# A two-layer fp32 transformer trunk on one core: layer 0's first output tokens loaded into the old pool, the last projection cut into six single tiles and five pairs, and layer 1's conditioning tied to its slots

## The chip, the cores and the metric

The kernel runs on one core of one Trainium2 chip. The metric is device time in microseconds (us) of one execution, given as the median of several runs. Besides, one execution was taken with the hardware profiler; its timeline is the source of all times of single instructions.

The engines are named as in the profile: PE is TensorE (matrix products), DVE is VectorE, ACT is ScalarE, POOL is GpSimd, SP is SyncE, which here does nothing but issue DMAs. SPq is SP's queue. "L247" is line 247 of the kernel before.

## The reference

One inference step of a trunk of two layers over 640 tokens of width 2048: 512 latent tokens and 128 context tokens. Each layer does this (the mixers' insides are left out):

```
for layer in (0, 1):
    shift, scale, gate = split(silu(cond) @ ada_w[layer] + ada_b[layer], 3)
    h = rms_norm(x, norm_g) * (1 + scale) + shift
    p = h @ w_in[layer]                     # the input projection
    o = concat(mixer 1(p), mixer 2(p))      # attention, gated conv
    o = o * silu(gate paths of p)
    x = x + gate * (o @ w_out[layer])       # the output projection
```

Layer 0 mixes with a banded attention and a gated convolution, layer 1 with a differential attention and an attention with rotary positions. `cond` has two rows, one for the latent tokens and one for the context tokens, so "conditioning" below means two products of a vector with a 2048 x 6144 matrix in each layer. Everything is fp32. The result is x of the last layer, with the context tokens' new keys and values.

## The kernel before, in words

**Tiles and products.** Tokens lie along the free axis in two halves of 320, features along the partitions in 16 blocks k of 128. An fp32 product is made of three fp32r products: each operand is split into a high part and a low part (`split`, L215 on ACT for the high part and L216 on DVE for the low one), and TensorE adds hi x hi, hi x lo and lo x hi (L247, L248, L249 in `proj_q`). An output tile is 128 features x 640 tokens in two PSUM banks (`pa`, `pb`): 16 blocks x 3 products x 2 halves = 96 matmuls. Its weights come in four quarters of four blocks each (256 KB), loaded by SP (`load_raw`, L228, tile `raw`) and split (`split_w`, tiles `wh` and `wl`); the pool of these tiles has four buffers of each, so a load waits for an older split and a split for matmuls that are done with its buffer. Within a tile, a quarter is 24 matmuls.

**The order of the work.** The program is written as Python generators that take turns: `run_tiles` walks through the tiles of a projection, and at the end of each quarter calls `slot`, which advances whatever is queued (`prep`: what follows a finished tile; `attn`: an attention head or the forms below; `fill`: a conditioning block). A scheduler then orders the instructions of each engine by its own model of time, so that neighbouring pieces of work may change places, where buffers and data allow it. Pools of tiles are opened and closed by hand; a tile in a new pool must wait for the old pool's tiles that lay there.

**Leads.** The first three tiles of a projection are leads (`run_tiles`, first loop). They run side by side through the quarters, because the tokens' blocks are made only now: before a quarter's matmuls, `make_h(k)` loads and splits block k. In the output projection the quarters are taken in the order 0, 2, 1, 3.

**The output projection** (`project_out`). It has 16 tiles n. Three are leads; one more, number N_SINGLE-1, is done singly, its token half 1 first and half 0 afterwards; the other 12 tiles are done as six pairs (`run_pairs`). A pair computes two tiles with seven products of half the depth and half the tokens instead of eight: 7 x 24 = 168 matmuls (L494, L495, L496, tile `pq`) against 192 for two single tiles. For it, sums of token blocks are needed, the forms: `forms` (L1018 on) loads blocks j and j+8 once more from DRAM (`w<-yd`, L1028), makes three sums and one more of them on DVE and splits the three into tiles T0 to T7. It is a generator with eight steps in the queue `attn`. The fourth sum (`t1`) is split in place over the tokens' half 1 when the fourth single tile's half 1 is done. The pairs' weights come in half columns (`load8`, L406, tag `w8`, four buffers); the forms' loads use the same four buffers.

**The tokens of the output projection.** The attention and the gates leave their results y (16 blocks) in DRAM as `yd` (`save_y`, L794, on POOL's queue). `y0_maker` (L1134) is layer 0's `make_h`: at k = 0 it closes the pool "even", opens "mid", allocates two tiles for the norm's sums, and starts the forms; `late_yin` (L1062, load at L1064) then loads each block into one of three buffers with the tag `xr` in the new pool and splits it. Layer 1's counterpart `y1_maker` already loads blocks 0 to 3 and 8 to 11 into buffers of the old pool (L1375). `y_maker` (L797) makes such a function for given tags of the pool that is current. In layer 0's attention the tags q0h, q0l, q1h and q1l hold the split q of the heads.

**What follows a tile.** In layer 1, each finished tile is added to the residual (L1059), then `rows_out` transposes it back to rows (L523 on PE, five transposes), copies it (L1381) and writes it out.

**Conditioning.** Layer 1's last four blocks of conditioning columns are made on DVE while layer 1's input projection runs (`ada_on_dve`, called `fill1`): for each block, 64 multiply-adds of half width (L187, in two accumulators `acc0` and `acc1`; the weights `adaw` loaded at L181 in three buffers), summed over the partitions by PE at the end (L193). `slot` advances the block by FILL1 = 0.9 steps a quarter from the 24th quarter on. Nothing but the buffers holds a block's DVE operations at the place where they are written.

**Layer 1's heads.** When a key tile is done, its rows are transposed on PE, squared on ACT (L548), scaled and rotated on DVE (L550 to L568, tile `m`), and transposed back on PE (L523).

Of the kernel before, what the change touches and what calls it, by code (L numbers as in the profile page):

```python
# [20 lines left out]
P = 128  # L21
D = 2048
KT = D // P
# [30 lines left out]
def trunk_kernel(ctx: ExitStack, tc: tile.TileContext, I: dict, O: dict):  # L54
# [114 lines left out]

    def ada_on_dve(blocks, tags, parts=1):  # L170

        wt, wd = tags[2:5], 512 // parts
        bufs = 3 if wt[0] == wt[1] else 1
        for l, cb in blocks:
            ap = pools["cur"]
            acc = [ap.tile([P, 512], F32, tag=tags[c], name=f"acc{c}", bufs=1) for c in range(2)]
            for i in range(KT * parts):
                kt, h = i % KT, i // KT
                w = ap.tile([P, wd], F32, tag=wt[i % 3], name="adaw", bufs=bufs)
                c0 = cb * 512 + h * wd  # L180
                nc.sync.dma_start(w, I["ada_w"][l, kt * P:(kt + 1) * P, c0:c0 + wd])  # L181
                for c in range(2):
                    a = acc[c][:, h * wd:(h + 1) * wd]
                    if kt == 0:
                        V.tensor_scalar(a, w, sT[:, kt, c:c + 1], None, ALU.mult)
                    else:
                        V.scalar_tensor_tensor(out=a, in0=w, scalar=sT[:, kt, c:c + 1], in1=a,  # L187
                                               op0=ALU.mult, op1=ALU.add)
                yield
# [36 lines left out]
    def load_raw(w_ap, col, qd, js=(0, 4)):  # L226
# [3 lines left out]
        return raw  # L230

    def split_w(raw):
        wh = wpool.tile(raw.shape, F32R, tag="wh", name="wh")
        wl = wpool.tile(raw.shape, F32R, tag="wl", name="wl")
        split(wh, wl, raw)
        return wh, wl

# [544 lines left out]
    fill0 = ada_on_dve(ada_rest[:N_FILL0], ("acc0", "acc1", "adaw", "adaw", "adaw", "z"))  # L782
    fill1 = ada_on_dve(ada_rest[N_FILL0:], ("acc0", "acc1", "adaw", "adaw", "adaw", "adaw"), 2)

# [225 lines left out]

    N_SINGLE = 4
    room = [tables[:, i * HALF:(i + 1) * HALF] for i in range(4)]
# [61 lines left out]
    def project_out(l, maker, finish, last, tail):  # L1074
# [11 lines left out]

        go_on = run_tiles([(n * P, job(n)) for n in range(N_SINGLE - 1)], w, maker, order=(0, 2, 1, 3))

        n = N_SINGLE - 1
        parts = [split_w(load_raw(w, n * P, qd)) for qd in range(4)]  # L1090
        go_on()
        pp = new_pp(0)
        for hv in (HV[1:], HV[:1]):
            for qd in range(4):
                proj_q(pp, parts[qd], qd, qd, hv)
                advance(attn, 2)
                go_on()
            if hv == HV[1:]:
                drain(attn)
                for j in range(8):  # L1100
                    hi, lo = hs[j]
                    split(hi[:, HALF:NT], lo[:, HALF:NT], t1[j])
        while go_on():
            pass
        prep.append(job(n)(pp))
        advance(prep, 1)

# [4 lines left out]
        def begin(p):  # L1112
            for t in range(2):
                res_load(l, N_SINGLE + 2 * p + t)

        def part(p, t, h, src):
            res_sum(l, N_SINGLE + 2 * p + t, src, CS[1:] if h else CS[:1])

        seen = set()

        def done(p, t, h, src):
            n = N_SINGLE + 2 * p + t
            part(p, t, h, src)
            if n >= KT - 2:
                last(t, h)
            elif n in seen:
                prep.append(later(n))
            seen.add(n)

        run_pairs([(n * P, (n + 1) * P) for n in range(N_SINGLE, KT, 2)], w,  # L1130
                  {"B11": half_of(0, 0), "T1": half_of(0, 1), "B21": half_of(8, 0), "B22": half_of(8, 1),
                   "T2": form_of(0), "T3": form_of(1), "T4": form_of(2)}, room, begin, part, done, tail)
        drain(prep)


    def y0_maker(k):
        if k == 0:
            close("even")
# [320 lines left out]
```

## Time and profile before

| what | value |
|---|---|
| runs | 2344.29, 2342.13, 2342.52 us |
| median | 2342.52 us |
| the profiled execution | 2347.92 us |
| its span (first to last instruction) | 2345.9 us |
| granted TensorE clock, mean | 0.994 of full speed |
| TensorE busy | 2286.9 us (97% of the span), 15900 matmuls |
| DVE, ACT, POOL busy | 67%, 40%, 6% |
| DMA | 321.92 MB, mean 137 GB/s |

How to read it: the times in the prediction's rows are counted from the span's start. A row of the timeline has start, duration, engine, line, operation, what is written `<-` what is read, and in brackets how long the engine had been idle before, and whose end it waited for. A row "x3" stands for three instructions one after the other. A row of the stretches has the busy time of each engine with its number of instructions, then the granted clock and the DMA engines' share and rate. A matmul's duration is longer than its distance to the next one, because they are pipelined.

Layer 0's output projection begins at about 921 us, layer 1's loads its first tokens from 2112 us on. Layer 1's input projection begins at about 1145 us.

### The profile page before, as it was taken

How to read it: one execution, taken by the hardware profiler on the slowest of the kernel's cores; microseconds unless marked ns; L12 is line 12 of the kernel's file. 1: busy time of each engine (PE TensorE's matmuls, PEld its weight loads, DVE VectorE, ACT ScalarE, POOL GpSimd, SP SyncE). 2: the span in 40 equal slices, each digit the busy share in tenths (PEclk: the TensorE clock that was granted, in tenths of full speed). 3: DMA queues.
4: the chain of work that ended last, by engine and by line, in shares of the span. 5: the costliest groups of instructions: out<-in, count | busy, mean ns of one | idle time of the engine just before them, and what ended most of it. 6: DMA issues, size and time to landing. Idle time of an engine off the chain costs nothing.

```text
span 2345.9 us, 41233 instructions
## 1 busy us (share of the span) xinstructions
PE 2286.9 (97%) x15900; PEld 2207.9 (94%) x15900; DVE 1577.8 (67%) x3187; ACT 932.9 (40%) x1934; POOL 129.7 (6%) x175
## 2 busy tenths in 40 slices
PE   6999999999999998999999999999999999999999
PEld 3789999999999998999989999999999999999999
DVE  4458886786866663888886445755855754568776
ACT  4325442433422222544553443444334444445343
POOL 0001000000000000000010100101000001000101
PEclk9999999999999999999999999999999999999999
DMA  9984545435355544844442222413423312128542
GB/s 325 327 266 141 157 117 170 138 117 170 106 172 155 154 136 127 274 140 129 157 135 84 80 74 71 139 55 97 120 72 92 106 46 82 46 74 282 165 122 69
DMA packets 386209, 321.92 MB, mean 137 GB/s; under 512 B 18033, under 2 KB 327854, under 8 KB 385502
## 3 DMA queue, kind: packets, MB, share of 16 engines
q1 hardware_dynamic: 378448, 290.96, 40.7%
q0 software_dynamic: 7024, 28.12, 3.3%
q8 instruction: 125, 2.05, 0.4%
q14 instruction: 70, 0.57, 0.1%
q10 hardware_dynamic: 542, 0.22, 0.0%
HBM read 290.79 MB, written 28.44 MB: 136 GB/s over the span
## 4 chain that ended last, share of the span: by engine, by line
PE 87%; DMA 5%; DVE 4%; issue 2%; ACT 2%; SPq 1%; POOL 0%; ACTq 0%; DVEq 0%; POOLq 0%
PE pa L247 10%; PE pb L247 10%; PE pb L248 10%; PE pb L249 10%; PE pa L248 10%; PE pa L249 10%; PE pq L494 4%; PE pq L496 4%; PE pq L495 4%; PE T L672 2%; DMA yin<-yd 2%; PE S L684 1%; PE S L686 1%; PE S L685 1%; DMA ada<-in_ada_w 1%
## 5 line engine op out<-in xcount | busy, mean ns | idle before, releaser
L215 ACT ACTIVATE wh<-raw 128x512 fp32r<-128x512 f32 (+1 forms) x478 | 298.5, 625 | 792.0 <-PE pb L248 655.0
L247 PE MATMUL pa<-h,wh 128*128 128x320 f32 x1728 | 552.0, 320 | 10.6 <-ACT h L215 7.9
L216 DVE TENSOR_TENSOR wl<-raw,wh 128x512 fp32r<-128x512 f32 (+1 forms) x478 | 326.5, 683 | 348.3 <-ACT wh L215 321.7
L248 PE MATMUL pa<-h,wh 128*128 128x320 f32 x1728 | 538.5, 312 | 2.8 <-DVE h L216 2.8
L249 PE MATMUL pa<-h,wl 128*128 128x320 f32 x1728 | 536.3, 310 | 0.0
L247 PE MATMUL pb<-h,wh 128*128 128x320 f32 x1728 | 535.8, 310 | 0.0
L249 PE MATMUL pb<-h,wl 128*128 128x320 f32 x1728 | 535.7, 310 | 0.0
L248 PE MATMUL pb<-h,wh 128*128 128x320 f32 x1728 | 535.1, 310 | 0.0
L187 DVE SCALAR_TENSOR_TENSOR acc<-adaw,sT,acc 128x512 f32<-128x512 f32 (+1 forms) x600 | 358.2, 640 | 16.3 <-DMA adaw<-in_ada_w 15.6
L247 PEld LDWEIGHTS pa<-h,wh 128*128 128x128 f32 x1728 | 326.5, 189 | 30.1 <-issue 14.9
L248 PEld LDWEIGHTS pa<-h,wh 128*128 128x128 f32 x1728 | 327.2, 189 | 8.5 <-issue 4.2
L249 PEld LDWEIGHTS pb<-h,wl 128*128 128x128 f32 x1728 | 325.0, 188 | 2.9 <-issue 2.9
L249 PEld LDWEIGHTS pa<-h,wl 128*128 128x128 f32 x1728 | 326.2, 189 | 1.3 <-issue 1.2
L247 PEld LDWEIGHTS pb<-h,wh 128*128 128x128 f32 x1728 | 325.3, 188 | 0.9 <-issue 0.4
L248 PEld LDWEIGHTS pb<-h,wh 128*128 128x128 f32 x1728 | 325.1, 188 | 0.1
L658 ACT ACTIVATE p<-S,nm,rq 128x768 f32<-128x768 f32 (+3 forms) x120 | 101.3, 844 | 114.2 <-DVE nm L653 80.0
L496 PE MATMUL pq<-h,wl 128*128 128x320 f32 x384 | 119.2, 311 | 3.1 <-DVE wl L216 3.1
L494 PE MATMUL pq<-h,wh 128*128 128x320 f32 x384 | 120.5, 314 | 0.3 <-DVE xr L1059 0.3
L495 PE MATMUL pq<-h,wh 128*128 128x320 f32 x384 | 119.1, 310 | 0.0
L651 DVE TENSOR_REDUCE nm<-S 128x1 f32<-128x768 f32 (+3 forms) x120 | 92.0, 767 | 16.0 <-PE S L686 14.9
L215 ACT ACTIVATE pth<-T 128x512 fp32r<-128x512 f32 (+1 forms) x132 | 66.2, 533 | 72.5 <-PE T L672 72.5
L495 PE MATMUL pq<-T,wh 128*128 128x320 f32 x288 | 88.8, 308 | 0.0
(294 smaller groups left out, 3446.6 us busy)
## 6 DMA issues: line engine op xcount, KB each, us to landing
raw<-in_od_w_in SPq DMA_DIRECT2D x208, 256.0 KB, 2.8
raw<-in_ev_w_in SPq DMA_DIRECT2D x202, 256.0 KB, 3.0
adaw<-in_ada_w SPq DMA_DIRECT2D x192, 256.0 KB, 2.9
ada<-in_ada_w SPq DMA_DIRECT2D x16, 2048.0 KB, 10.1
adaw<-in_ada_w SPq DMA_DIRECT2D x128, 128.0 KB, 2.3
yd<-y POOLq DMA_DIRECT2D x34, 320.0 KB, 3.0
yin<-yd SPq DMA_DIRECT2D x32, 320.0 KB, 4.4
w<-yd SPq DMA_DIRECT2D x32, 320.0 KB, 4.3
```

The source lines that it names most:

```text
L187: V.scalar_tensor_tensor(out=a, in0=w, scalar=sT[:, kt, c:c + 1], in1=a, op0=ALU.mult, op1=ALU.add)
L215: A.activation(hi, x, AF.Copy)
L216: V.tensor_sub(lo, x, hi)
L247: PE.matmul(ps, wh[:, i, :], hi[:, sl], start=(j == js[0] if alone else (pos == 0 and j == 0)), stop=False)
L248: PE.matmul(ps, wh[:, i, :], lo[:, sl], start=False, stop=False)
L249: PE.matmul(ps, wl[:, i, :], hi[:, sl], start=False, stop=(j == js[1] - 1 if alone else (pos == 3 and j == 3)))
L494: PE.matmul(ps, wh[:, j, :], hi, start=(h == 0 and j == 0), stop=False)
L495: PE.matmul(ps, wh[:, j, :], lo, start=False, stop=False)
L496: PE.matmul(ps, wl[:, j, :], hi, start=False, stop=(h == 1 and j == 3))
L651: V.tensor_reduce(nm, s, axis=AX.X, op=ALU.max, negate=True)
L658: A.activation(p[:, 0:n], s, AF.Exp, scale=rsc, bias=nm, accum_out=l)
L672: PE.transpose(t[:, i * P:(i + 1) * P], p, ident)
```

## The change

It has three parts.

1. **Layer 0's tokens.** `y0_maker` makes blocks 0 to 3 with a `y_maker` over the tags q0h, q0l, q1h, q1l of the old pool. Closing "even", opening "mid", the norm's tiles and the start of the forms move from k = 0 to k = 8, the first block of the second quarter in the order 0, 2, 1, 3.
2. **Singles and pairs.** N_SINGLE becomes (4, 6): layer 0 keeps four single tiles and six pairs, layer 1 has six and five. The single tiles from number 3 on are now a loop that loads the weights four quarters ahead and splits them three quarters ahead (SPLIT_AHEAD); the last of them is done in two halves as before.
3. **The tie.** At the start of each block of layer 1's conditioning on DVE, the first column of both accumulators is written with a column of the weight tile that was split last (`mark`). The products overwrite it. The block's operations can therefore not be ordered ahead of that split.

```diff
--- before.py
+++ after.py
@@ -167,13 +167,18 @@
         add_bias(l, cb, red, h, n)
         ada_done(l, cb, h, n)
 
-    def ada_on_dve(blocks, tags, parts=1):
+    def ada_on_dve(blocks, tags, parts=1, tie=lambda: None):
+
 
         wt, wd = tags[2:5], 512 // parts
         bufs = 3 if wt[0] == wt[1] else 1
         for l, cb in blocks:
             ap = pools["cur"]
             acc = [ap.tile([P, 512], F32, tag=tags[c], name=f"acc{c}", bufs=1) for c in range(2)]
+            mark = tie()
+            if mark is not None:
+                for c in range(2):
+                    V.tensor_copy(acc[c][:, 0:1], mark)
             for i in range(KT * parts):
                 kt, h = i % KT, i // KT
                 w = ap.tile([P, wd], F32, tag=wt[i % 3], name="adaw", bufs=bufs)
@@ -229,10 +234,13 @@
                           .rearrange("(k p) n -> p k n", p=P))
         return raw
 
+    mark = [None]
+
     def split_w(raw):
         wh = wpool.tile(raw.shape, F32R, tag="wh", name="wh")
         wl = wpool.tile(raw.shape, F32R, tag="wl", name="wl")
         split(wh, wl, raw)
+        mark[0] = wl[:, 0, 0:1]
         return wh, wl
 
     HV = ((0, slice(0, HALF)), (1, slice(HALF, NT)))
@@ -780,7 +788,8 @@
 
     ada_rest = [(0, cb) for cb in range(8, 12)] + [(1, cb) for cb in (4, 0, 5, 1, 6, 2, 7, 3, 8, 9, 10, 11)]
     fill0 = ada_on_dve(ada_rest[:N_FILL0], ("acc0", "acc1", "adaw", "adaw", "adaw", "z"))
-    fill1 = ada_on_dve(ada_rest[N_FILL0:], ("acc0", "acc1", "adaw", "adaw", "adaw", "adaw"), 2)
+    fill1 = ada_on_dve(ada_rest[N_FILL0:], ("acc0", "acc1", "adaw", "adaw", "adaw", "adaw"), 2,
+                       lambda: mark[-1])
 
     ydram = [dram.tile([P, NT], F32, name=f"yd{k}") for k in range(KT)]
     x0dram = [dram.tile([P, 4 * NT + 1], F32, name=f"x0d{g}") for g in range(4)]
@@ -1008,7 +1017,7 @@
     for _ in fill0:
         pass
 
-    N_SINGLE = 4
+    N_SINGLE = (4, 6)
     room = [tables[:, i * HALF:(i + 1) * HALF] for i in range(4)]
     W_OUT = [I["ev_w_out"][0], I["od_w_out"][0]]
     T, t1 = [], []
@@ -1084,26 +1093,39 @@
                 finish(n)
             return f
 
-        go_on = run_tiles([(n * P, job(n)) for n in range(N_SINGLE - 1)], w, maker, order=(0, 2, 1, 3))
-
-        n = N_SINGLE - 1
-        parts = [split_w(load_raw(w, n * P, qd)) for qd in range(4)]
+        n0 = N_SINGLE[l]
+        go_on = run_tiles([(n * P, job(n)) for n in range(3)], w, maker, order=(0, 2, 1, 3))
+
+
+        quarters = [(n * P, qd) for n in range(3, n0) for qd in range(4)]
+        raws, parts = [], []
+
+        def run_ahead(t):
+            while len(raws) < min(t + 4, len(quarters)):
+                raws.append(load_raw(w, *quarters[len(raws)]))
+            while len(parts) < min(t + SPLIT_AHEAD, len(quarters)):
+                parts.append(split_w(raws[len(parts)]))
+
+        run_ahead(0)
         go_on()
-        pp = new_pp(0)
-        for hv in (HV[1:], HV[:1]):
-            for qd in range(4):
-                proj_q(pp, parts[qd], qd, qd, hv)
-                advance(attn, 2)
-                go_on()
-            if hv == HV[1:]:
-                drain(attn)
-                for j in range(8):
-                    hi, lo = hs[j]
-                    split(hi[:, HALF:NT], lo[:, HALF:NT], t1[j])
-        while go_on():
-            pass
-        prep.append(job(n)(pp))
-        advance(prep, 1)
+        for n in range(3, n0):
+            pp, t = new_pp((n - 3) % 2), 4 * (n - 3)
+            for hv in ([HV] if n < n0 - 1 else [HV[1:], HV[:1]]):
+                for qd in range(4):
+                    proj_q(pp, parts[t + qd], qd, qd, hv)
+                    run_ahead(min(t + qd + 1, len(quarters) - 3))
+                    advance(attn, 1 if len(hv) == 2 else 2)
+                    go_on()
+                if len(hv) == 1 and hv[0][0]:
+                    drain(attn)
+                    for j in range(8):
+                        hi, lo = hs[j]
+                        split(hi[:, HALF:NT], lo[:, HALF:NT], t1[j])
+            while n == n0 - 1 and go_on():
+                pass
+            drain(prep)
+            prep.append(job(n)(pp))
+            advance(prep, 1)
 
         def later(n):
             yield
@@ -1111,15 +1133,15 @@
 
         def begin(p):
             for t in range(2):
-                res_load(l, N_SINGLE + 2 * p + t)
+                res_load(l, n0 + 2 * p + t)
 
         def part(p, t, h, src):
-            res_sum(l, N_SINGLE + 2 * p + t, src, CS[1:] if h else CS[:1])
+            res_sum(l, n0 + 2 * p + t, src, CS[1:] if h else CS[:1])
 
         seen = set()
 
         def done(p, t, h, src):
-            n = N_SINGLE + 2 * p + t
+            n = n0 + 2 * p + t
             part(p, t, h, src)
             if n >= KT - 2:
                 last(t, h)
@@ -1127,14 +1149,18 @@
                 prep.append(later(n))
             seen.add(n)
 
-        run_pairs([(n * P, (n + 1) * P) for n in range(N_SINGLE, KT, 2)], w,
+        run_pairs([(n * P, (n + 1) * P) for n in range(n0, KT, 2)], w,
                   {"B11": half_of(0, 0), "T1": half_of(0, 1), "B21": half_of(8, 0), "B22": half_of(8, 1),
                    "T2": form_of(0), "T3": form_of(1), "T4": form_of(2)}, room, begin, part, done, tail)
         drain(prep)
 
 
+    make_y0 = y_maker(("q0h", "q0l", "q1h", "q1l"), NT)
+
     def y0_maker(k):
-        if k == 0:
+        if k < 4:
+            return make_y0(k)
+        if k == 8:
             close("even")
             open_pool("mid")
             st["acc"] = pools["cur"].tile([P, NT], F32, name="acc")
```

## The prediction

> **What bounds the kernel now.** I read the page first, then busy time by stretches of the span, then TensorE's waits, then the timeline around each wait. The page comes first:
>
> ```profile
> span 2345.9 us, 41233 instructions
> ...
> PE 2286.9 (97%) x15900; PEld 2207.9 (94%) x15900; DVE 1577.8 (67%) x3187; ACT 932.9 (40%) x1934; POOL 129.7 (6%) x175
> ...
> PE 87%; DMA 5%; DVE 4%; issue 2%; ACT 2%; SPq 1%; POOL 0%; ACTq 0%; DVEq 0%; POOLq 0%
> ```
>
> TensorE is busy for 97% of the span and carries 87% of the chain that ended last. So only two things can move the time: TensorE's own work, or the 59 us in which it waits, with the slow clock that follows. The stretches show where these sit (columns: from:to, length, busy time and instructions of each engine, granted clock, DMA share, GB/s):
>
> ```profile
> 921.00:977.00 56.00, 46.09 (x293) 44.31 (x292) 44.58 (x75) 27.32 (x39) 1.08 (x2) 0.94 0.88 283
> 1000.00:1020.00 20.00, 20.00 (x138) 20.00 (x137) 17.21 (x30) 9.04 (x15) 1.08 (x2) 1.00 0.49 148
> 1195.00:1225.00 30.00, 25.98 (x166) 24.15 (x165) 24.96 (x57) 16.06 (x45) 5.18 (x5) 0.89 0.39 117
> 1205.00:1210.00 5.00, 5.00 (x21) 4.96 (x20) 3.49 (x8) 3.48 (x7) 0.00 (x0) 0.51 0.56 163
> 1466.00:1510.00 44.00, 42.98 (x302) 40.63 (x301) 38.27 (x90) 20.59 (x47) 5.60 (x4) 1.00 0.49 146
> 2160.00:2192.00 32.00, 26.32 (x171) 25.47 (x170) 22.67 (x44) 14.03 (x28) 5.17 (x8) 0.95 0.75 228
> 2175.00:2180.00 5.00, 5.00 (x36) 5.00 (x36) 3.30 (x6) 2.83 (x5) 0.00 (x0) 1.00 1.11 355
> 2185.00:2190.00 5.00, 4.69 (x23) 4.39 (x22) 1.82 (x4) 0.85 (x2) 0.00 (x0) 0.66 0.37 108
> ```
>
> At full clock and with no wait, 138 matmuls take 20 us: 0.145 us each. By that price three stretches lose time, and each part of the change touches one of them:
> - 921 to 977 (layer 0's three lead tiles): 293 matmuls are worth 42.5 us, so 13.5 us of 56 are lost: 9.9 idle and 3.6 at a low clock.
> - 1195 to 1225 (layer 1's first head): 4.0 idle, and about 2.2 at the clock of 0.51 in 1205 to 1210 (21 matmuls where 34 fit): 6.2 us.
> - 2160 to 2192 (layer 1's output projection): 5.7 idle, and 1.3 to 1.7 behind it, where the clock is 0.66 (23 matmuls in 4.69 us): about 7.2 us.
>
> TensorE's waits from 905 on name what ended them (summed us, times, longest):
>
> ```profile
> PE pa L247 <- ACT h L215: 7.9, 2, 7.5
> PE T L523 <- DVE m L568: 4.9, 3, 3.2
> PE pq L496 <- DVE wl L216: 3.1, 1, 3.1
> PE T L523 <- ACT ot L1381: 2.3, 1, 2.3
> ```
>
> **The change part by part. Part 1, layer 0's tokens.** The timeline of the first wait, and the transfers ahead of it:
>
> ```profile
> 639.54 0.38 SPq L228 DMA_DIRECT2D raw<-in_ev_w_in  x1
> 644.28 0.38 SPq L228 DMA_DIRECT2D raw<-in_ev_w_in  x1
> 901.45 21.48 SPq L228 DMA_DIRECT2D raw<-in_ev_w_out  x7
> 920.99 0.31 PE L249 MATMUL pb<-h,wl 128*128 128x320 f32 x1
> 923.87 1.29 SPq L1064 DMA_DIRECT2D yin<-yd  x3
> 927.97 0.74 ACT L215 ACTIVATE h<-yin 128x640 fp32r<-128x640 f32 x1 [5.83 <-DMA yin<-yd]
> 928.76 0.63 PE L247 MATMUL pa<-h,wh 128*128 128x320 f32 x1 [7.46 <-ACT h L215]
> 932.81 0.74 ACT L215 ACTIVATE h<-yin 128x640 fp32r<-128x640 f32 x1 [1.70 <-DMA yin<-yd]
> ```
>
> The last matmul of the input projection starts at 920.99. The token blocks are asked for only at 923.87, when the old pool has closed. The first split reaches ACT at 927.97, so TensorE waits 7.46 us and starts again slowly.
>
> In the changed program, blocks 0 to 3 are asked for in the old pool, in the slots of the attention's q tiles. In the order in which it is built, these four loads stand on SP among the weight loads around 640 us. They wait there for TensorE's last use of q:
>
> ```profile
> L686 PE MATMUL S<-k0h,q1l x1: 282/282/282, 643.0 to 643.0; 128*128 128x256 f32 x1
> ```
>
> Weight loads that stand behind these waits can be held for at most some 3.5 us (639.54 to 643.0). SP's raw loads run up to five quarters ahead of TensorE, and a quarter of a tile is 24 matmuls or 3.5 us, so I cost this at nothing. Without that cover it is 3.5 us. The eight splits of blocks 0 to 3 stand on ACT and DVE ahead of 921; they cover the first quarter of the leads: 72 matmuls, 10.4 us.
>
> What is late next is block 8, the first that needs the new pool. A ninth weight load now stands ahead of it on SP (eight before), and that one needs a weight buffer that comes free only with the first lead's 24 matmuls, at about 924.9. So block 8 is asked for at about 926.4, 2.5 us later than the first block before. Before, request to first matmul took 4.9 us: block 8 is ready at 931.3, when TensorE needs it at 921.1 + 10.4 = 931.5. No gap there. Block 11 comes some 4.9 us behind it (927.97 to 932.81 for four blocks), at 936.2, and is needed after 24 matmuls of its quarter, at 935.0: 1.3 us late. For the last two groups I take the idle time that these leads have now beside the first wait: 9.9 - 7.5 = 2.4. So about 4 us of loss stay: **-9.5 us** (bounds: -13.5 if all of it goes; -6.0 if a whole wait of 7.46 like the present one comes back in the later groups).
>
> The pool's closing and the forms move one quarter, 10.4 us, later. In the leads' stretch DVE is busy for 44.6 of 56 us, much of it with the forms; if they end a full 10 us behind 977, that is 987. They are needed by the third product of the first pair: leads' end at 967 (9.5 earlier), 96 matmuls of the fourth single, 48 of two products, so 967 + 144 x 0.145 = 988. I cost it at nothing; without that cover each us of delay counts in full, some 3.5 if a quarter is missing.
>
> **Part 3, the tie.** What stands around the second head of layer 1:
>
> ```profile
> 1193.03 0.71 PE L523 MATMUL T<-ident,stg 128*128 128x128 f32 x5
> 1193.45 2.49 DVE L187 SCALAR_TENSOR_TENSOR acc<-adaw,sT,acc 128x256 f32<-128x256 f32 x6 [0.39 <-DMA adaw<-in_ada_w]
> 1195.81 0.19 ACT L548 ACTIVATION_READ_ACCUMULATOR junk<-T 128x1 f32 x1
> 1196.82 1.28 DVE L187 SCALAR_TENSOR_TENSOR acc<-adaw,sT,acc 128x256 f32<-128x256 f32 x3 [0.28 <-DMA adaw<-in_ada_w]
> 1198.01 0.68 DVE L550 TENSOR_TENSOR kg<-T,gain_rows 128x512 f32<-128x512 f32 x1
> 1203.43 0.69 DVE L568 TENSOR_TENSOR m<-m,m 128x512 f32<-128x512 f32 x1
> 1204.17 1.11 PE L523 MATMUL T<-ident,m 128*128 128x128 f32 x4 [3.17 <-DVE m L568]
> L193 PE MATMUL T<-acc,ones x32: 379/391/404, 1466.4 to 1974.2; 128*32 128x256 f32 x32
> ```
>
> The key's rows are in PSUM at 1193.7 and ACT has squared them at 1196.0, but DVE begins with them (L550) at 1198.01: the conditioning's products of block 1 stand between. TensorE waits 3.17 us for the chain's end and runs at half clock afterwards. The result of this block is read first at 1466.4 (L193).
>
> The change adds two one-column copies a block, eight in all on DVE. The trace has no such copy; it lies between nothing and the 0.68 us of the 128x512 operation L550, so under 5.4 us of DVE in all, at places where DVE waits for its inputs anyway: nothing on TensorE. They read the newest weight split, which DVE itself has made earlier in its order, so nothing queues behind a wait. In the built order the 64 products of block 1 leave 1189 to 1250 and stand at about 1308 to 1366; blocks 2 to 4 stay. There are 100 us left until 1466. Without these products L568 ends near 1201, when TensorE needs it. So 6.2 us go, less 0.7 for the rest of the chain. In the new place they stand beside other heads. The nearest row is block 2's own, 1466 to 1510, with 1.0 us idle on TensorE: +1.0. Sum **-4.5 us** (bounds: -6.2 if nothing comes back, 0 if the new heads wait as this one did).
>
> **Part 2, six singles and five pairs in layer 1.** A pair costs 7 x 24 = 168 matmuls, two singles 192: +24 x 0.145 = **+3.5 us** of TensorE, certain. What it may take away:
>
> ```profile
> 2167.07 0.77 PE L523 MATMUL T<-ident,xr 128*128 128x128 f32 x5 [2.26 <-ACT ot L1381]
> 2174.81 10.78 SPq L406 DMA_DIRECT2D w<-in_od_w_out  x3
> 2184.12 0.42 PE L496 MATMUL pq<-h,wl 128*128 128x320 f32 x1 [3.12 <-DVE wl L216]
> 2185.71 0.41 PE L494 MATMUL pq<-h,wh 128*128 128x320 f32 x1 [0.31 <-DVE xr L1059]
> ```
>
> The pairs' weights can be loaded only when the forms free their buffers, from 2174.81, at 355 GB/s; the first pair's second operand is then 3.12 us late. Two more singles put 192 matmuls, 27.8 us, between the forms and the first pair: the 3.12, the 0.31 and the 1.7 of slow clock behind them go (-5.1). The leads' row transposes now stand 24 matmuls apart instead of 12, which I take to save 1.3 of the 2.26. Sum +3.5 - 5.1 - 1.3 = **-2.9 us** (bounds: -3.9 with all of the 2.26, +3.5 if the waits only move to the new first pair).
>
> By the Trainium skill ("TensorE: Matmul & The Clock Gate", "Part 1: The HAM clock gate"), the clock halves after an idle window of about 3.4 us. The trace disagrees: 0.51 is granted right behind a wait of 3.17 us. By that rule of the Trainium skill the slow clock behind the waits of 3.17 and 3.12 us would not go away with them, and the sum would be 2.2 + 1.7 = 3.9 us smaller; I go by the rows.
>
> **Sum.** -9.5 - 4.5 - 2.9 = -16.9 us. The profiled execution took 2347.92 us (span 2345.9), which gives 2331.0. The median of the runs, 2342.52, lies 5.4 below it; with the same step: **2325.6, taken as 2326 us**.
>
> **The rivals.**
> - A, the tokens come no faster: the loads of blocks 8 to 15 and the forms' own ten loads share one queue, so the wait moves to the second quarter. For it: SP's order, weights behind splits behind matmuls. Against it: 10.4 us of cover. Part 1 gives -3.5: 2342.5 - 10.9 = 2331.6.
> - B, the conditioning's block takes its cost along: its 64 products delay another head just as much. Against it: the analogue's 1.0 us. Part 3 gives 0: 2330.1.
> - C, the singles cost their matmuls and the first pair waits all the same, since its loads still stand behind something on SP. Part 2 gives +3.5: 2332.0.
> - D, slower: at the leads, each of the three late groups of blocks now waits in turn, because the weight load ahead of it on SP waits for a split, which waits for a buffer that TensorE frees, which itself waits for tokens. Each round costs one wait like the present one with its slow clock, 7.5 + 1.2 = 8.7 us: 26 instead of 13.5, +12.6. With the other parts +5.2: 2347.7. It decides from 8.5 us a round (three make 25.6; 25.6 - 13.5 - 7.4 = 4.7). Against it: the present leads lose only 2.4 us idle in those same three groups.
> - E, the change doesn't do what it says: A and C together with little of part 3, the same waits at other places: about 2340 to 2343.
>
> **How the numbers follow.** Forecast 0.60; A 0.11, B 0.07, C 0.07; D 0.07; E 0.08. A measurement of this kernel can tell about 0.2%, 4.7 us, from no change. Forecast, A, B and C are faster by more: 0.85; E within: 0.08; D slower: 0.07. The range begins where every part reaches its best bound, -13.5 - 6.2 - 3.9 = -23.6: 2319, taken as 2318; it ends at 2338, where A and C fall together (-3.5 - 4.5 + 3.5 = -4.5). D and E are left out.
>
> **What would show it.** Part 1: no TensorE wait above 2 us at 921, one of 1 to 2 us near 935, and over 320 matmuls in 921 to 977. Part 3: no wait of L523 for L568 near 1204, the clock at 1.00 in 1205 to 1210, and the products at about 1300 to 1360 with under 2 us idle on TensorE. Part 2: the first pair without a wait, 24 matmuls more in the singles. Wrong would make it: waits of 3 us or more behind 931, each with a clock near 0.5; or one near 1310 to 1370.

## The result, and the profile after

Six runs of each kernel on the same chip: 2333.21 us (2330.09 to 2336.12) after, 2343.07 us (2340.01 to 2350.96) before. The ratio over all runs is 0.9953, 95% interval 0.9936 to 0.9970: 11 us faster (7 to 15), where 16.9 were forecast; the medians alone differ by 9.9. The profiled execution took 2336.12 us (span 2334.1), the slowest of the six, against 2347.92 before: 11.8 less.

The page of the kernel after:

```profile
span 2334.1 us, 41243 instructions
...
PE 2288.0 (98%) x15924; PEld 2207.8 (95%) x15924; DVE 1566.7 (67%) x3177; ACT 928.8 (40%) x1927; POOL 130.6 (6%) x175
```

24 matmuls more, TensorE busy 1.1 us longer, and yet 11.8 us less: 59 us of waiting have become 46. TensorE's five largest waits from 905 on (what waited, what ended it: summed us, times, longest):

```profile
PE T L531 <- DVE m L576: 3.6, 5, 1.7
PE pa L255 <- ACT h L220: 3.1, 3, 1.3
PE T L531 <- ACT ot L1407: 1.5, 2, 1.3
PE T L1212 <- POOL r L1208: 1.5, 1, 1.5
PE T L531 <- DVE k0l L221: 1.4, 2, 0.8
```

The lines have moved: L220 and L221 are L215 and L216 of before, L192 is L187, L255 is L247, L531 is L523, L558 is L550, L576 is L568, L502 is L494, L1068 is L1059, L1407 is L1381. The other runs have numbers of their own, a few apart. The waits of 7.5 us for the first tokens and of 3.1 us at the first pair are gone. The wait for the key's chain (L576) is still the longest in sum; it is spread over five places. The stretches of the kernel after (length, busy us and instructions of PE, PEld, DVE, ACT, POOL, clock, DMA share, GB/s):

```profile
921.00:977.00 56.00, 52.40 (x339) 51.05 (x339) 43.24 (x76) 27.53 (x42) 2.17 (x4) 0.97 0.84 273
1180.00:1290.00 110.00, 108.19 (x756) 105.39 (x755) 60.08 (x128) 51.04 (x123) 9.06 (x11) 1.00 0.23 68
1290.00:1370.00 80.00, 76.88 (x532) 74.39 (x531) 57.19 (x132) 33.46 (x83) 10.11 (x11) 1.00 0.43 130
2150.00:2215.00 65.00, 63.49 (x438) 62.76 (x438) 40.52 (x71) 25.08 (x47) 7.77 (x12) 1.00 0.61 188
```

and the last three of them in the kernel before:

```profile
1180.00:1290.00 110.00, 105.95 (x718) 103.53 (x717) 81.37 (x182) 49.30 (x118) 9.10 (x10) 0.97 0.37 109
1290.00:1370.00 80.00, 79.86 (x559) 77.68 (x559) 36.56 (x77) 35.87 (x91) 8.90 (x11) 1.00 0.27 79
2150.00:2215.00 65.00, 58.48 (x391) 57.37 (x390) 50.98 (x92) 27.66 (x52) 6.45 (x10) 0.97 0.68 207
```

The length less PE's busy time is TensorE's idle time. In the leads 9.9 us idle became 3.6, and 46 matmuls more were done in the same 56 us. Around the first head 4.0 became 1.8. In the stretch 1290 to 1370 it went the other way: 0.1 became 3.1, with 27 matmuls fewer. This is where the products of block 1 now stand; DVE's busy time there rose from 36.6 to 57.2, about as much as it fell in the stretch before. In the last projection 6.5 became 1.5.

### The profile page after: what moved, and what is told of

Same layout as the page of the kernel before. It is cut to its first block, busy times and chain, and to the rows that moved or that the text cites. A ratio compares the mean times of both kernels' runs of the same rounds, so it can differ in the third digit from the quotient of the medians.

```text
span 2334.1 us, 41243 instructions
## 1 busy us (share of the span) xinstructions
PE 2288.0 (98%) x15924; PEld 2207.8 (95%) x15924; DVE 1566.7 (67%) x3177; ACT 928.8 (40%) x1927; POOL 130.6 (6%) x175
## 4 chain that ended last, share of the span: by engine, by line
PE 89%; DMA 4%; DVE 3%; ACT 2%; issue 1%; SPq 1%; POOL 0%; ACTq 0%; DVEq 0%; POOLq 0%
PE pa L255 10%; PE pb L255 10%; PE pb L256 10%; PE pb L257 10%; PE pa L256 10%; PE pa L257 10%; PE pq L502 4%; PE pq L504 4%; PE pq L503 4%; PE T L680 2%; PE S L692 1%; DMA yin<-yd 1%; PE S L694 1%; PE S L693 1%; PE T L157 1%
## 5 line engine op out<-in xcount | busy, mean ns | idle before, releaser
L220 ACT ACTIVATE wh<-raw 128x512 fp32r<-128x512 f32 (+1 forms) x484 | 302.3, 626 | 798.4 <-PE pb L256 653.7
L221 DVE TENSOR_TENSOR wl<-raw,wh 128x512 fp32r<-128x512 f32 (+1 forms) x484 | 330.4, 683 | 351.2 <-ACT wh L220 324.5
L255 PE MATMUL pa<-h,wh 128*128 128x320 f32 x1760 | 560.9, 319 | 4.4 <-ACT h L220 3.1
L256 PE MATMUL pa<-h,wh 128*128 128x320 f32 x1760 | 547.3, 312 | 1.1 <-DVE h L221 1.1
L257 PE MATMUL pa<-h,wl 128*128 128x320 f32 x1760 | 546.0, 310 | 0.0
L257 PE MATMUL pb<-h,wl 128*128 128x320 f32 x1760 | 545.5, 310 | 0.0
L255 PE MATMUL pb<-h,wh 128*128 128x320 f32 x1760 | 545.4, 310 | 0.0
L256 PE MATMUL pb<-h,wh 128*128 128x320 f32 x1760 | 544.9, 310 | 0.0
L192 DVE SCALAR_TENSOR_TENSOR acc<-adaw,sT,acc 128x512 f32<-128x512 f32 (+1 forms) x600 | 357.9, 639 | 17.5 <-DMA adaw<-in_ada_w 16.8
L255 PEld LDWEIGHTS pa<-h,wh 128*128 128x128 f32 x1760 | 332.1, 189 | 23.9 <-issue 15.1
L256 PEld LDWEIGHTS pa<-h,wh 128*128 128x128 f32 x1760 | 332.6, 189 | 6.3 <-issue 4.2
L257 PEld LDWEIGHTS pb<-h,wl 128*128 128x128 f32 x1760 | 330.9, 188 | 2.9 <-issue 2.9
L255 PEld LDWEIGHTS pb<-h,wh 128*128 128x128 f32 x1760 | 331.0, 188 | 0.9 <-ACT h L882 0.4
L256 PEld LDWEIGHTS pb<-h,wh 128*128 128x128 f32 x1760 | 331.0, 188 | 0.1
L502 PE MATMUL pq<-h,wh 128*128 128x320 f32 x352 | 110.0, 313 | 0.4 <-DVE xr L1068 0.4
L503 PE MATMUL pq<-h,wh 128*128 128x320 f32 x352 | 108.8, 309 | 0.0
L504 PE MATMUL pq<-h,wl 128*128 128x320 f32 x352 | 108.4, 309 | 0.0
L659 DVE TENSOR_REDUCE nm<-S 128x1 f32<-128x768 f32 (+3 forms) x120 | 91.9, 766 | 15.9 <-PE S L694 14.8
L220 ACT ACTIVATE pth<-T 128x512 fp32r<-128x512 f32 (+1 forms) x132 | 66.0, 534 | 71.5 <-PE T L680 71.4
L503 PE MATMUL pq<-T,wh 128*128 128x320 f32 x264 | 81.5, 309 | 0.0
```

What stands on the lines that cost most here:

```text
L220: A.activation(hi, x, AF.Copy)
L221: V.tensor_sub(lo, x, hi)
L255: PE.matmul(ps, wh[:, i, :], hi[:, sl], start=(j == js[0] if alone else (pos == 0 and j == 0)), stop=False)
L256: PE.matmul(ps, wh[:, i, :], lo[:, sl], start=False, stop=False)
L257: PE.matmul(ps, wl[:, i, :], hi[:, sl], start=False, stop=(j == js[1] - 1 if alone else (pos == 3 and j == 3)))
L502: PE.matmul(ps, wh[:, j, :], hi, start=(h == 0 and j == 0), stop=False)
```

## The experiments

Each was timed beside the kernel before on one chip, and the chips differ from run to run, so runs are compared by their ratios. The runs of one part alone are the kernel before with that part; all others are the kernel after with the edit shown, where `...` stands for lines left out. A ratio is to the kernel before, over all runs, with its 95% interval in brackets; us worked out from a ratio are taken of 2343, and two kernels are compared by the difference of their ratios.

**The parts one by one.** First the tokens alone:

```diff
+make_y0 = y_maker(("q0h", "q0l", "q1h", "q1l"), NT)
+
 def y0_maker(k):
-    if k == 0:
+    if k < 4:
+        return make_y0(k)
+    if k == 8:
...
```

> Part 1 alone, put into the kernel before. Theory after the two profiles: the first wait (7.46 us) goes, about 1 us comes back in the later groups of blocks, and the slow clock behind stays: -6.5 us (2336 to 2338 where before is 2343), with some 3.5 us idle in the leads. Rival, the size of the forecast: -9.5 us, with little more than 2 us idle and no slow clock left. If the gain of the whole change came from elsewhere, it is under 4 us.

Ratio 0.9960 (0.9948 to 0.9972): -9.4 us (-12.2 to -6.6). It is the forecast's size, and more than I had read out of the two profiles. The leads and, within them, the stretch of the later groups in this kernel, then the later groups in the kernel after:

```profile
921.00:977.00 56.00, 53.67 (x356) 51.87 (x355) 44.83 (x78) 28.73 (x45) 2.16 (x4) 1.00 0.86 277
935.00:977.00 42.00, 39.68 (x265) 38.55 (x264) 37.83 (x68) 23.77 (x37) 1.62 (x3) 1.00 0.92 293
```

```profile
935.00:977.00 42.00, 39.94 (x261) 39.08 (x260) 36.67 (x66) 22.79 (x35) 1.63 (x3) 0.97 0.85 275
```

In the later groups idle time is nearly the same, but the kernel after shows a clock of 0.97 and the other 1.00. In the whole leads this kernel is idle for 2.3 us and does 63 matmuls more than the kernel before, worth 9.1 us at the 0.145 us of the prediction; the kernel after is idle for 3.6 and does 46 more, worth 6.7. So the profile of the kernel after, taken of its slowest execution, shows less than part 1 is worth.

The singles alone:

```diff
-    N_SINGLE = 4
+    N_SINGLE = (4, 6)
```

(with the loop over the single tiles that belongs to it)

> Part 2 alone. Theory: 24 matmuls more cost 3.5 us; the first pair's waits (3.1 + 0.3), the slow clock behind them (1.7) and some of the transposes' 2.26 go: -2 to -3 us, no wait above 0.7 us at the first pair, 288 + 192 single matmuls of layer 1 at 0.147 us each. Rival C: the wait only moves to the new first pair: +3.5 us.

Ratio 0.9988 (0.9979 to 0.9997): -2.8 us (-4.9 to -0.7). The waits of TensorE from 2140 to the end, all that there are:

```profile
PE T L1423 <- DVE xr L1068: 0.6, 1, 0.6
PE T L531 <- ACT ot L1403: 0.2, 1, 0.2
PE T L1423 <- issue: 0.2, 1, 0.2
```

No wait at the first pair is left, and the transposes' 2.26 us are 0.2.

The tie alone:

```diff
+            mark = tie()
+            if mark is not None:
+                for c in range(2):
+                    V.tensor_copy(acc[c][:, 0:1], mark)
...
```

(with the mark set in `split_w` and handed to layer 1's blocks, as in the change)

> Part 3 alone. Theory after the profiles: the first head's loss of about 5.5 us goes (the wait of 3.17 and its slow clock), and the products of the moved block delay another head about 140 us later by 1.7 + 0.6 us and a little elsewhere: -1 to -3 us in all. Rival, the size of the forecast: -4.5 us. Rival B: 0.

Ratio 1.0003 (0.9993 to 1.0013): nothing, +0.7 us (-1.6 to +3.0). The stretch of the new place, and the waits for the key's chain from 905 to 2300:

```profile
1290.00:1370.00 80.00, 76.73 (x526) 74.33 (x525) 58.42 (x138) 34.02 (x86) 9.35 (x10) 0.98 0.42 124
```

```profile
PE T L530 <- DVE m L575: 4.2, 5, 2.2
```

3.3 us are idle in 1290 to 1370, and the clock is below 1.00: the wait of 3.17 us at the first head has become one of 2.23 us at 1351.20 and some smaller ones, here even with slow clock behind them. Of the sum of 4.9 us before, 4.2 are left. This stretch does 33 matmuls fewer than in the kernel before (526, 559), 4.8 us by their price; the one from 1180 to 1290 does 31 more (749, 718), 4.5 us. The two cancel.

Parts 1 and 2 together, the mark given as none:

```diff
-                       lambda: mark[-1])
+                       lambda: None)
```

> Parts 1 and 2 without the tie. If the parts add up: the gain of the whole change less that of the tie alone, so -8 to -10 us from before by the theory (-6.5 - 2.5), -12 by the forecast (-9.5 - 2.9). The first head of layer 1 should again wait for L568's counterpart by about 3 us, with the clock at half behind it.

Ratio 0.9950 (0.9938 to 0.9962): -11.7 us (-14.5 to -8.9), the whole gain of the change (0.9953). The first head waits again:

```profile
1194.42 1.11 PE L531 MATMUL T<-ident,m 128*128 128x128 f32 x4 [2.77 <-DVE m L576]
```

So the parts add up: -9.4 - 2.8 + 0.7 = -11.5, against -11.0 measured for all three. The tie earns nothing at this place.

**Why the tie earns nothing.** The timeline of DVE in the kernel after, at the second head that block 1 now meets, and what TensorE makes of it:

```profile
1332.68 2.65 DVE L192 SCALAR_TENSOR_TENSOR acc<-adaw,sT,acc 128x256 f32<-128x256 f32 x6
1333.80 0.71 PE L531 MATMUL T<-ident,stg 128*128 128x128 f32 x5
1336.09 1.27 DVE L192 SCALAR_TENSOR_TENSOR acc<-adaw,sT,acc 128x256 f32<-128x256 f32 x3 [0.15 <-DMA adaw<-in_ada_w]
1337.28 0.68 DVE L558 TENSOR_TENSOR kg<-T,gain_rows 128x512 f32<-128x512 f32 x1
1338.14 0.48 DVE L192 SCALAR_TENSOR_TENSOR acc<-adaw,sT,acc 128x256 f32<-128x256 f32 x1
1340.43 0.48 DVE L192 SCALAR_TENSOR_TENSOR acc<-adaw,sT,acc 128x256 f32<-128x256 f32 x1
1342.70 0.68 DVE L576 TENSOR_TENSOR m<-m,m 128x512 f32<-128x512 f32 x1
1343.44 0.66 PE L531 MATMUL T<-ident,m 128*128 128x128 f32 x4 [1.68 <-DVE m L576]
```

It is the picture of 1193 to 1204 over again: nine products stand ahead of the chain's first operation (L558), the last three of them behind a wait of 0.15 us for their load, and two more within it. At the head before this one (1304) nine stand as well; its waits of 0.51, 0.18 and 0.62 us and this one of 1.68 make up nearly all of the stretch's idle time.

The number of products does not set the wait. The same nine and two stand at block 2's own head in the kernel before, in the stretch that the forecast took as its analogue (first three rows). The last two rows show a head with no product, from the run below with the blocks 12 quarters later:

```profile
1485.87 0.71 PE L523 MATMUL T<-ident,stg 128*128 128x128 f32 x5
1488.51 0.69 DVE L550 TENSOR_TENSOR kg<-T,gain_rows 128x512 f32<-128x512 f32 x1
1494.67 0.66 PE L523 MATMUL T<-ident,m 128*128 128x128 f32 x4 [0.84 <-DVE m L568]
1301.32 0.71 PE L531 MATMUL T<-ident,stg 128*128 128x128 f32 x5
1303.56 0.69 DVE L558 TENSOR_TENSOR kg<-T,gain_rows 128x512 f32<-128x512 f32 x1 [0.83 <-ACT junk L556]
```

TensorE has 48 matmuls of the projection, 7 us, between the key rows' first transposes (`stg`) and the ones back (`m`), at each of these heads. Without products the chain begins on DVE 2.24 us after the first transposes, and TensorE does not wait for its end. With them it begins 2.64 us after at block 2, 3.48 here, 4.98 at the first head of the kernel before: 0.40, 1.24 and 2.74 us late. The waits of 0.84, 1.68 and 3.17 us are that lateness plus 0.43 or 0.44. Most of this rest is the chain itself, which takes 6.1 us with two products within and 5.7 without. The head at 1345 of the tie alone fits as well (4.03 us after, wait 2.23). Why the same nine products end sooner or later against the transposes, no run isolates.

To see that the products are the cause, I left out 56 of the block's 64 (the expectation's 62 is a miscount) and kept its loads and sums; this kernel leaves the block's result unfinished:

```diff
-                    else:
+                    elif parts == 1 or cb != 8 or kt == 1:
                         V.scalar_tensor_tensor(out=a, in0=w, scalar=sT[:, kt, c:c + 1], in1=a,
```

> The changed kernel, with 62 of the 64 DVE products a half-width block of conditioning needs (all but those of the first two steps of each half) left out in the first tied block, its loads and sums kept. Theory (the block takes its cost along): in the stretch where it now stands the waits of 1.7 and 0.6 us for the key's chain go, idle TensorE between 1298 and 1413 falls from 3.2 to about 0.3 us, as it was there before; 3 us faster than the changed kernel. Rival: the waits there come of something else (loads, transposes), and stay.

```profile
1290.00:1370.00 80.00, 79.86 (x554) 77.88 (x553) 34.21 (x68) 34.50 (x83) 8.57 (x10) 1.00 0.29 87
```

Idle time falls from 3.1 to 0.1 us; ratio 0.9942 (0.9928 to 0.9956), 2.6 us below the kernel after where 3 were expected, though the intervals overlap. In the trace, the products are what TensorE pays for.

Next, the block spread out: each step tied to its slot.

```diff
-            mark = tie()
-            if mark is not None:
-                for c in range(2):
-                    V.tensor_copy(acc[c][:, 0:1], mark)
...
+                mark = tie()
+                if mark is not None:
+                    V.tensor_copy(w[:, 0:1], mark)
                 c0 = cb * 512 + h * wd
```

> The changed kernel, with each step of the four blocks tied to its own slot, and not the block's beginning alone: the mark is written into the first column of the step's weight tile ahead of its load. In the order as built, 1 to 2 products stand before a key's chain in place of 5 or 6. Theory (three products in a row ahead of the chain, with their wait for the load, are what makes TensorE wait): the waits of 1.7 and 0.6 shrink below 1 us, also at the other heads: 2 to 4 us faster than the changed kernel. Rival: the products of one block cost the same wherever they stand, or the 128 added copies eat the gain: no change, or up to 2 us slower.

Ratio 0.9952 (0.9938 to 0.9966): no change, as the rival had it. Two stretches of this kernel, then the second one of the kernel after:

```profile
1290.00:1370.00 80.00, 79.38 (x551) 77.24 (x551) 48.22 (x117) 34.07 (x85) 9.33 (x11) 1.00 0.36 110
1370.00:2100.00 730.00, 725.41 (x5073) 707.49 (x5072) 465.66 (x1117) 313.14 (x681) 48.35 (x59) 1.00 0.29 86
```

```profile
1370.00:2100.00 730.00, 727.33 (x5088) 709.88 (x5087) 445.11 (x981) 313.01 (x680) 48.26 (x59) 1.00 0.28 83
```

In 1290 to 1370 the idle time falls from 3.1 to 0.6, but in 1370 to 2100 it rises from 2.7 to 4.6. Of the ten key chains from 1180 to 2000, eight now have products in the 6 us ahead of them, two to four each; in the kernel after it is three, with nine each. The run also adds 128 copies of 0.149 us each, 19 us of DVE, and does not tell which of the two the rise comes from.

Then the blocks kept whole and moved: a start 12 quarters later is to put every block between the chains.

```diff
-FILL1_FROM = 24
+FILL1_FROM = 36
```

> The changed kernel with layer 1's conditioning begun at the 36th quarter in place of the 24th, so that each tied block stands 12 quarters (some 42 us) later; in the order as built no product stands in or right before a key's chain any more. Theory (the block costs only where it meets a key's chain): idle TensorE in the stretch 1298 to 1413 falls from 3.2 to about 0.3 us, at the later heads by another 0.5 to 1: 3 to 4 us faster than the changed kernel, ratio to before near 0.9938. Rival (64 products cost the same wherever they stand, as the run with every step tied left open): within 1 us of the changed kernel.

```profile
1290.00:1370.00 80.00, 79.86 (x556) 77.87 (x555) 47.41 (x105) 34.02 (x84) 9.71 (x11) 1.00 0.37 111
1370.00:2100.00 730.00, 727.70 (x5092) 709.79 (x5090) 453.58 (x1017) 314.44 (x684) 47.30 (x59) 1.00 0.29 85
```

0.1 us idle in the first stretch and 2.3 in the second, 2.4 where the kernel after has 5.8; DVE is busy for 501 us in the two together, in the kernel after for 502. In this trace none of the ten key chains has a product in the 6 us ahead of it or inside it. So it is not the work but the meeting with a chain that costs. Ratio 0.9941 (0.9924 to 0.9958), 2.8 us below the kernel after; the intervals overlap, so the gain in time is likely and not shown, while the stretches show the waits gone.

**What is left in the leads.** The forms begun at the third quarter:

```diff
             st["sq"] = pools["cur"].tile([P, NT], F32, name="sq")
+        if k == 4:
             attn.append(forms())
```

> The changed kernel with the forms begun at the third quarter of the leads (k = 4), not at the second (k = 8). Theory: in the second quarter the DMA share is 0.99, so the forms' own loads delay the blocks 9 to 11; without them the wait of 1.1 + 0.5 us near 932 and the slow clock behind it go, 1.5 to 3 us less in the leads; it comes back as long as the forms are late for the first pair. Rival: blocks 9 to 11 are late for the weights' sake: the waits stay.

```profile
935.00:977.00 42.00, 40.79 (x273) 39.82 (x273) 37.84 (x68) 22.48 (x35) 1.63 (x3) 1.00 0.95 300
977.00:1000.00 23.00, 19.33 (x122) 19.08 (x121) 19.45 (x32) 9.14 (x16) 0.54 (x1) 0.93 0.69 194
```

```profile
PE pq L502 <- DVE xr L1068: 3.7, 1, 3.7
```

The leads lose less (273 matmuls against 261), but TensorE then waits 3.7 us at the first pair, with slow clock. Ratio 0.9969 (0.9959 to 0.9979): about 4 us worse than the kernel after, with intervals that overlap. The forecast's claim that the forms' delay is covered holds for one quarter (0.4 us of wait at the first pair of the kernel after) and not for two.

The forms' loads on another queue:

```diff
-                nc.sync.dma_start(ts[i], ydram[j + 8 * i])
+                nc.gpsimd.dma_start(ts[i], ydram[j + 8 * i])
```

> The changed kernel with the forms' loads issued from POOL's queue in place of SP's; the same bytes. Theory (the rate of transfers is the limit near 930, not the order on SP): blocks 9 to 11 come no earlier, the leads lose as much as now, within 1 us. Rival (blocks stand behind forms' loads that wait for buffers): the waits of 1.3 and 0.75 us near 949 and 960 go, 2 us less.

Ratio 1.0006 (0.9994 to 1.0018): the whole gain is gone, which neither side had expected. The waits of TensorE from 905 to 1000:

```profile
PE pa L256 <- DVE h L221: 4.7, 4, 3.6
PE pa L255 <- ACT h L220: 2.4, 1, 2.4
PE pq L502 <- DVE xr L1068: 1.9, 1, 1.9
```

The longest wait is now for the low part of a block, on DVE. The forms' loads land later here than on SP (median 5.1 us from issue to landing, 4.3 in the kernel after), DVE waits 1.38 us for one at 962 in the middle of a form's sums, and the block's split stands behind it. The edit moves the forms' loads of both layers, and layer 1 loses about as much. The largest of the waits from 2100 on, and the stretch there:

```profile
PE T L531 <- DVE xr L1068: 4.4, 2, 3.1
2150.00:2215.00 65.00, 59.94 (x391) 58.33 (x389) 40.77 (x76) 22.67 (x41) 10.79 (x18) 0.95 0.68 208
```

The row transposes of layer 1's first tiles wait for sums that stand behind late forms on DVE. The stretch has 47 matmuls fewer than in the kernel after, 6.8 us; the leads and the 23 us behind them have 59 fewer (432, 491), 8.6 us. Whether SP's order or the rate of transfers sets the residue of 3.6 us in the leads is not settled by this run.

Eight blocks early:

```diff
+    make_y8 = y_maker(("P",), 640)
...
+        if 8 <= k < 12:
+            return make_y8(k)
-        if k == 8:
+        if k == 4:
             close("even")
```

> The changed kernel with blocks 8 to 11 also loaded into the old pool, in the buffers of the attention's p, and pool and forms changed at the third quarter (k = 4). Theory (the second quarter is limited by the rate of transfers of blocks and forms together): the leads shorten from 48.8 to 43 to 45 us; the forms then end late for the first pair, and 2 to 4 us come back in the fourth single tile, as with the forms begun later: 0 to 3 us faster than the changed kernel. Rival: with eight blocks in place the forms run faster and nothing comes back: 4 to 6 us faster.

```profile
915.00:935.00 20.00, 20.00 (x138) 20.00 (x137) 12.09 (x20) 9.73 (x16) 0.54 (x1) 1.00 0.63 210
935.00:977.00 42.00, 41.11 (x281) 40.85 (x279) 37.01 (x69) 21.47 (x35) 1.62 (x3) 1.00 0.93 289
977.00:1000.00 23.00, 20.46 (x127) 20.23 (x128) 19.26 (x31) 7.81 (x14) 0.54 (x1) 0.93 0.55 160
```

From 915 to 935 TensorE is now busy throughout; the forms are late for the fourth single and the first pair, and 3.4 us are idle behind that (0.9 in 935 to 977 and 2.5 in 977 to 1000), with slow clock. Ratio 0.9971 (0.9958 to 0.9984): some 4 us slower than the kernel after, with intervals that overlap, where 0 to 3 faster were expected. The trace does not account for this: it is of the fastest of the run's eight executions (2333.4 us, median 2336.3), and from 921 to 1000 it has 12 matmuls more than the kernel after. What the other executions lose stays open.

**The price of a single.** Eight singles and four pairs:

```diff
-    N_SINGLE = (4, 6)
+    N_SINGLE = (4, 8)
```

> The changed kernel with eight single tiles and four pairs in layer 1. Theory: nothing is left to win at the first pair, so the one price of a pair made single stays: 24 matmuls x 0.146 = +3.5 us against the changed kernel (ratio to before near 0.9968), layer 1's singles and pairs together longer by that. Rival: more time for the forms and the weights also takes away the waits of the row transposes (1.5 us): +2 us or less.

Ratio 0.9975 (0.9963 to 0.9987), 5.2 us slower than the kernel after, with intervals that take in 3.5. The row transposes keep waits of 1.2 us in all, where the kernel after has 1.5, so hardly anything is won for it.

**The two later steps together.** Block 8 also early, so that pool and forms change at k = 9, and the blocks 12 quarters later (`make_y8` as in the run with eight blocks):

```diff
+        if k == 8:
+            return make_y8(k)
-        if k == 8:
+        if k == 9:
             close("even")
...
-FILL1_FROM = 24
+FILL1_FROM = 36
```

> The changed kernel with two steps more: block 8 is loaded into the old pool too (in a buffer of the attention's p), so pool and forms change at k = 9; and the conditioning begins at the 36th quarter. Theory: the later conditioning keeps its 3 us (idle between 1298 and 1413 under 0.4 us); the leads lose the wait near 931 (1 to 1.5 us, with its slow clock), and the forms, less than one block later, end in time for the first pair: 3 to 5 us faster than the changed kernel, ratio to before 0.993 to 0.994. Rival: the waits of the third and fourth group grow by as much as the second's shrinks, as they did where eight blocks were early: ratio 0.994 to 0.9955.

Ratio 0.9932 (0.9919 to 0.9946), 2328.14 us against 2343.32: -15.9 us, the lowest ratio of all runs and 4.9 us below the kernel after, with intervals that still overlap. The leads and the stretch of block 1:

```profile
935.00:977.00 42.00, 41.70 (x283) 41.18 (x282) 40.06 (x73) 24.99 (x38) 1.62 (x3) 1.00 0.93 297
977.00:1000.00 23.00, 22.44 (x152) 22.06 (x151) 20.76 (x35) 9.03 (x15) 0.54 (x1) 1.00 0.67 194
1290.00:1370.00 80.00, 79.86 (x555) 77.88 (x554) 49.42 (x108) 34.57 (x84) 9.17 (x10) 1.00 0.39 117
```

0.3 us idle in the later groups, 0.6 at the first pair, 0.1 at block 1: the forms are in time, and block 1's loss is gone. Of the leads' loss 1.2 us in 921 to 977 are left, 0.9 of them between 930 and 935, in short waits.

## Why the prediction was right, and where it was not

**Part 1 was right in sign and size.** -9.5 forecast, -9.4 measured alone (-12.2 to -6.6). Its steps held: the loads of blocks 0 to 3 among the weights cost nothing (TensorE is busy for all of 636 to 660 in both kernels); the blocks were split ahead of the leads; block 8 was asked for late, some 5.3 us into the leads, and was in time; a later block of its group kept TensorE waiting, 1.09 and 0.45 us near 931 to 933 where 1.3 was forecast (it was block 9, not 11); and 3.6 us of idle time were left where 3.7 (1.3 + 2.4) were forecast. That close an agreement is luck: with the tokens alone only 2.3 us were left, nothing of the 1.3 occurred (TensorE busy for 4.99 of 5 us in 930 to 935), and a wait of 1.7 us stood later. Rivals A and D did not occur: no wait of a whole round of 7.5 us came back. That the delayed forms stay covered held in the change, up to 0.4 us, and the run with a still later start shows how thin the cover is.

**Part 2 was right.** -2.9 forecast, -2.8 measured alone (-4.9 to -0.7). Rival C did not occur: no wait moved to the new first pair.

**Part 3 was wrong: the failed step is the "+1.0" for the products in their new place.** The forecast priced the moved block by the one other stretch in which a block stood (1466 to 1510, 1.0 us idle), and rival B, that "its 64 products delay another head just as much", was given 0.07. It is what happened. The first half of the part held: in 1180 to 1290 the idle time went from 4.0 to 1.8 us and the clock from 0.97 to 1.00, and 38 matmuls more fit in, 5.5 us by their price, which is the forecast's 6.2 - 0.7. The second half did not: in 1290 to 1370 the idle time went from 0.1 to 3.1 in the kernel after, 27 matmuls fewer or 3.9 us, and to 3.3, with slow clock, in the tie alone, 33 fewer or 4.8 us. So the term put at 1.0 is 4 to 5.

The price of a block is not a property of the block. It comes from the chains that it meets and from how late it lets each begin. The row chosen as the analogue had one such meeting, with the same nine products, but the chain there began 0.40 us late; at the new place there are two, and the second begins 1.24 us late. The traces do not say why. I had looked at where the block stood and not at what stood next to it.

With part 3 as measured (+0.7 in place of -4.5), the forecast's sum would have been -9.5 - 2.9 + 0.7 = -11.7; -11.0 was measured. The sign that was to make part 3 wrong, one wait of 3 us or more near 1310 to 1370, did not appear: the same loss came in four waits of 0.18 to 1.68 us. The one-column copies were costed rightly at nothing: they took 0.146 us each.

One sum in the prediction is off without consequence: where 34 matmuls fit and 21 ran, its own price gives 1.9 us of slow clock at the first head and not 2.2, so 5.9 in place of 6.2.

The range, 2318 to 2338, held the time of 2333.2, and the kernel became faster, as forecast. That the total came out inside the range is owed to its width: parts 1 and 2 made up all of the gain.

## What to carry to other kernels

Work that is pulled off one latency chain on a busy, in-order engine gains nothing where it delays another such chain as much: list the chains of the whole stage, before and after, and look at how late each one's first operation begins, not only at how much work stands before it. A move that fixes the visible wait can hand it to the next head at about the same price, and then the next step is to look for a place between the chains, as the start 12 quarters later did. And when a buffer that is free early lets a stage begin on time, ask what else was tied to the old start (here the forms): their cover is the next limit.

## What was unexpected of the hardware

Slow clock did not need a wait of 3 us. In the kernel after, it followed two short waits of 1.09 and 0.45 us that ended within 1 us of each other, at 931.77 and 932.63:

```profile
930.00:935.00 5.00, 3.46 (x19) 2.97 (x18) 3.21 (x6) 2.73 (x4) 0.00 (x0) 0.90 0.99 367
935.00:940.00 5.00, 5.00 (x29) 5.00 (x28) 3.48 (x6) 2.10 (x3) 0.00 (x0) 0.76 0.73 251
```

With the tokens alone, whose waits for ACT's splits in the leads reach 1.7 us, the clock stayed at 1.00 in 935 to 977 (the row is above). In the tie alone the wait of 2.23 us at 1351 was followed by a clock of 0.50 (1352 to 1354), while behind the wait of 2.26 us at 2167 in the kernel before it stayed at 1.00 (2165 to 2175). The Trainium skill ("TensorE: Matmul & The Clock Gate", "Part 1: The HAM clock gate") names an idle window of about 3.4 us as what halves the clock; the runs here do not agree, since less was enough. So the length of one wait did not decide it, and the one or two us that a slow stretch costs a single profile can be a matter of the execution: the median of the runs, or a second kernel with the same waits, is needed before it is put down to a change.
